# Four modulation jobs of block 2's last layer: from TensorE in block 2 to GpSimd in block 1

## The chip, the core and the metric

The kernel runs on one core of a Trainium2 chip. A core has TensorE (matmuls), VectorE, ScalarE and GpSimd, each with its own in-order queue of instructions, and SyncE, whose queue (SP) issues the DMAs here. The metric is the time of one execution on the device in microseconds; lower is better.

## What is computed

Two blocks of two layers each, on 256 tokens of 1024 features in fp32. Every layer is modulated by a vector `c`: a product of `silu(c)` with a 1024 x 3072 matrix gives shift, scale and gate. Block 1 has one modulation vector, block 2 two (latents and context). Cut to that:

```python
def hybrid_layer(x, c_silu, ...):                       # block 1, 2 layers
    shift, scale, gate = split(c_silu @ w_ada + b_ada, 3)
    u = rms_norm(x, norm_g) * (1 + scale) + shift
    z = u @ w_in                                        # then attentions a, b, c and their merge
    return x + gate * (merged @ w_out)

def mixer_layer(x, cx, c, c_ctx, ...):                  # block 2, 2 layers
    shift, scale, gate = split(silu(c) @ w_ada + b_ada, 3)
    shift_c, scale_c, gate_c = split(silu(c_ctx) @ w_ada + b_ada, 3)
    h = x * (1 + scale) + shift;  hc = cx * (1 + scale_c) + shift_c
    ...                                                 # h @ w_in, four mixers, w_out, layer norm
```

## The kernel before

**Weights.** All projections go through the same path. SP loads half a tile of weights (128 x 1024, 512 KB) into one of three buffers `wr` (`raw`, L222), ScalarE makes its rounded part `wh` (L114) and VectorE the rest `wl` (L115), with four buffers each, and TensorE multiplies three combinations of `wh`, `wl` with the split activations (`mm`, L107).

**Modulation.** The 3072 columns of a layer's modulation are worked out in the background by one of two kinds of jobs (`ada`). A *small job* takes 256 columns (12 to a layer): two loads of 512 KB, eight matmuls `ps<-wsp,cs` or `ps<-wr,cs`, a copy `adas`, two transposes, and two small VectorE instructions into `mod`. A *wide job* takes 512 columns (6 to a layer, so one stands for two small ones) and works on GpSimd: four loads (L324), each of which is multiplied by a column of `cs` (L330, L333) and added up in `acc` (L334); with two modulation vectors that makes 16 multiplications and 14 additions. Its `end` is eight matmuls of `acc` with ones (four with one vector) and one VectorE instruction. The first of the two products of a piece of weights goes into a tile `wc`, the second overwrites the weights. The loads of wide jobs go in turn into the two tiles `t3a` and `t3b` (`N.spare`).

**What sets the order.** The jobs stand in a list `bg`. After each of certain weight tiles (42 in a layer of block 1) `after_tile` adds `N.rate` to `N.due` and, for each whole unit, takes a job from the list, as long as more than `N.hold` are left. `end` of a wide job is put into `later` and run ten `after_tile`s on (six with one vector), or at a `flush`. At the start of layer 1 of block 1 `fill(4, ...)` takes four small jobs at once, whose eight loads go into the tiles `a4`, `a5`, `a6`, `g1`, `g2`, `g3`, `t3a` and `t3b`; they are to lie under the switch of layers. A scheduler then orders the instructions of each engine, so that code order is only a hint; on the chip each engine and SP follow that order strictly.

**The switch between the layers of block 1.** When the last output tile of layer 0 is done, ScalarE squares `xT`, TensorE sums the squares (`th,ones`, then `sel,cs`), VectorE scales the sum (L378), GpSimd takes its power -1/2 (`rc`, L379), VectorE makes a diagonal of it (`dg`, L382), TensorE spreads it (`dg,ones`), and VectorE and ScalarE make the split `u` (L524 to L526), with which the projections of layer 1 begin (`wh,uh`).

**Where the jobs are before.** In layer 0 of block 1: two wide jobs of its own gate and four of layer 1 (one vector each). In layer 1: four wide jobs for layer 0 of block 2. In block 2: the four last small jobs of its layer 0 (two of them at its start), and all twelve of its layer 1, so that 14 go through `wr`. Of the tags: `stg` is the tile in which block 1 stages its `bq` queries (L456); `w2` is used only by layer 1 of block 2.

Of the kernel before, what the change touches and what calls it, by code (L numbers as in the profile page):

```python
# [58 lines left out]
class Net:  # L59
# [185 lines left out]
    def run_later(self, now=False):  # L245

        left = []
        for n, f in self.later:
            if n > 0 and not now:
                left.append((n - 1, f))  # L250
                continue
            with self.tc.issue_after(self.last_mm):
                f()
        self.later = left
# [34 lines left out]
    def ada(self, l, blk):  # L289

        nc = self.nc
        nv = 1 if blk == 1 else 2
        wa = self.I["w_ada" if blk == 1 else "w_ada_2"][l]
        v0 = blk - 1
        mod = self.const.tile([128, 24, nv], F32, name=f"mod{blk}{l}")

        def load(n):
            return [self.raw(wa, k, n * 256, 256, True) for k in (0, 4)]

        def job(n, ws=None):  # L300
            ws = ws or load(n)
            bias = self.colB[:, 48 * (blk - 1) + 24 * l:48 * (blk - 1) + 24 * l + 24]
            p = self.P(self.pj, [128, 512])
            for k in range(8):
                g = 32 * (k % 4)
                self.mm(p[g:g + 32, :256], self.cs[:, k, :], ws[k // 4][:, k % 4, :], start=k < 4, stop=k >= 4)
            sb = self.W("adas", [128, 256], tag="score")
            nc.scalar.activation(sb, p[:, :256], AF.Copy)
            pc = self.P(self.tr, [128, 2, 4, 32])
            for j in range(2):  # L310
                self.T(pc[:, j].rearrange("p g v -> p (g v)"), sb[:, 128 * j:128 * j + 128])
            r = self.W("adar", [128, 2, nv])
            nc.vector.tensor_reduce(r, pc[:, :, :, v0:v0 + nv].rearrange("p j g v -> p j v g"), axis=AX.X, op=OP.add)
            nc.vector.scalar_tensor_tensor(mod[:, 2 * n:2 * n + 2, :], r, 0.5,
                                           bias[:, 2 * n:2 * n + 2][:, :, None].to_broadcast([128, 2, nv]),
                                           op0=OP.mult, op1=OP.add)
        def wide(n, tag):

            P = nc.gpsimd
            acc = self.K("acc", [128, 2, 512], tag=tag)  # L320
            for c in range(4):
                w = self.K("wsp", [128, 2, 512], tag=self.spare[self.nspare % len(self.spare)])
                self.nspare += 1
                nc.sync.dma_start(out=w, in_=wa[256 * c:256 * c + 256, 512 * n:512 * n + 512].rearrange(  # L324
                    "(k p) n -> p k n", p=128))
                for k in range(2):
                    for v in range(nv):
                        m = self.cs[:, 2 * c + k, v0 + v:v0 + v + 1]
                        if c == k == 0:
                            P.tensor_scalar(acc[:, v], w[:, k], m, None, op0=OP.mult)  # L330
                        else:
                            t = self.W("wc", [128, 512], tag="stg") if v + 1 < nv else w[:, k]
                            P.tensor_scalar(t, w[:, k], m, None, op0=OP.mult)  # L333
                            P.tensor_tensor(acc[:, v], acc[:, v], t, op=OP.add)  # L334

            def end():
                p = self.P(self.tr, [128, 4, 32])
                for j in range(4):
                    for v in range(nv):
                        self.mm(p[:, j, v:v + 1], acc[:, v, 128 * j:128 * j + 128], self.ones[:, 0:1])  # L340
                bias = self.colB[:, 48 * (blk - 1) + 24 * l:48 * (blk - 1) + 24 * l + 24]
                nc.vector.scalar_tensor_tensor(mod[:, 4 * n:4 * n + 4, :], p[:, :, :nv], 0.5,
                                               bias[:, 4 * n:4 * n + 4][:, :, None].to_broadcast([128, 4, nv]),
                                               op0=OP.mult, op1=OP.add)
            self.later.append((6 if nv == 1 else 10, end))

        return (mod, [lambda ws=None, n=n: job(n, ws) for n in range(12)], [lambda n=n: wide(n, ("s4", "w1")[n % 2]) for n in range(6)],
                load)

# [991 lines left out]
def build(ctx, tc, I, out):  # L1341
    N = Net(ctx, tc, I)
    nc = N.nc

    def flush(left=0):
        while len(N.bg) > left:
            N.bg.popleft()()
        N.run_later(True)

    N.load_consts()  # L1350
    mod, jobs, wide, load = N.ada(0, 1)
    N.spare = ["t3a", "t3b", "a1", "a2", "a3", "a4", "a5", "a6", "a7", "g1", "g2", "g3", "t1"]
    ws = {0: load(0)}
    N.ident = N.const.tile([128, 128], F32, name="ident")
    nc.sync.dma_start(out=N.ident, in_=I["ident"])
    ws[4] = load(4)
    xT = N.K("xT", [128, 8, 256])
    nc.sync.dma_start(out=xT, in_=I["x"])
    for n in range(4):
        for m in (n, n + 4):  # L1360
            jobs[m](ws.get(m))
    pre = {"idx": [N.raw(N.I["w_in"][0], k, OFF1["idx"], 256) for k in (0, 4)]}
    t = N.K("pre", [128, 8, 256], tag="t2")
    for k in (0, 4):
        nc.sync.dma_start(out=t[:, k:k + 4], in_=N.I["w_in"][0][k * 128:k * 128 + 512, :256].rearrange(
            "(k p) n -> p k n", p=128))
    pre["aq"] = [t[:, 0:4], t[:, 4:8]]
    t = N.K("pre", [128, 8, 68], tag="n2")
    nc.sync.dma_start(out=t, in_=N.I["w_in"][0][:, OFF1["idx"] + 256:OFF1["idx"] + 324].rearrange(
        "(k p) n -> p k n", p=128))  # L1370
    pre["iw"] = [t[:, 0:4], t[:, 4:8]]
    N.load_cs1()
    N.spare = ["t3a", "t3b"]
    N.bg.extend(wide[4:])
    for l in range(2):
        nmod, jobs, wide, _ = N.ada(1, 1) if l == 0 else N.ada(0, 2)
        N.bg.extend(wide[:4] + jobs[8:])
        N.hold = 4
        N.rate = 0.19 if l == 0 else 0.11
        N.due = 1.0  # L1380
        N.block1(l, xT, mod, pre if l == 0 else {})
        flush(4)
        mod = nmod
    X = N.halves("cT", ("t3a", "t3b"))
    for t, ks in X.parts():
        nc.sync.dma_start(out=t, in_=I["ctx_2"][:, ks])
    H, R = {}, {}

    def stream(l, s, x, r, g, b, mod):
        H[s] = N.pair("h" + s, {"x": ("uh", "ul"), "c": ("t1", "t2")}[s])  # L1390
        sc, bi = N.mod_cols(g, b, mod, 0 if s == "x" else 1)
        N.affine_split(H[s][0], H[s][1], x, sc, bi, r)
        if s == "x" or l == 0:
            R[s] = N.residual(x, r, g, b, f"res{s}{l}")

    stream(0, "c", X, None, None, None, mod)
    stream(0, "x", xT, N.rstd_row(xT, EPS), N.colA[:, 0:8], None, mod)
    nmod, jobs, _, _ = N.ada(1, 2)
    N.bg.extend(jobs)
    N.hold = 0  # L1400
    N.rate = 0.8
    ln = lambda l: (N.colA[:, 24 + 8 * l:32 + 8 * l], N.colA[:, 40 + 8 * l:48 + 8 * l])

    def context_done(x, r):
        flush()
        stream(1, "c", x, r, *ln(0), nmod)

    N.spare = None
    N.fill(2, ["a7", "g1", "g2", "g3"])
    x, r = N.block2(0, R, H, mod, context_done)  # L1410
    stream(1, "x", x, r, *ln(0), nmod)
    xT, r = N.block2(1, R, H, nmod, None)
    g, b = ln(1)
    for k in range(8):
        nc.vector.scalar_tensor_tensor(xT[:, k], xT[:, k], g[:, k:k + 1], r, op0=OP.mult, op1=OP.mult)
        nc.scalar.activation(xT[:, k], xT[:, k], AF.Identity, bias=b[:, k:k + 1])
        nc.sync.dma_start(out=out[:, k], in_=xT[:, k])
# [74 lines left out]
```

## Time and profile before

| | |
|---|---|
| median of 3 runs (lowest to highest) | 1353.47 us (1352.70 to 1354.14) |
| the profiled execution, its own time | 1352.58 us |
| its span in the trace | 1350.8 us |
| mean granted clock of TensorE | 0.972 |
| TensorE busy | 1277.5 us (95%) |
| VectorE, ScalarE, GpSimd busy | 908.9, 648.8, 393.9 us |

The span is shorter than the execution's own time, since it begins with the first instruction; differences within the trace are read in the span, and are compared with the times as differences. A busy TensorE says that matmuls were in flight, not that they ran at full speed.

### The profile page before, as it was taken

How to read it: one execution, taken by the hardware profiler on the slowest of the kernel's cores; microseconds unless marked ns; L12 is line 12 of the kernel's file. 1: busy time of each engine (PE TensorE's matmuls, PEld its weight loads, DVE VectorE, ACT ScalarE, POOL GpSimd, SP SyncE). 2: the span in 40 equal slices, each digit the busy share in tenths (PEclk: the TensorE clock that was granted, in tenths of full speed). 3: DMA queues.
4: the chain of work that ended last, by engine and by line, in shares of the span. 5: the costliest groups of instructions: out<-in, count | busy, mean ns of one | idle time of the engine just before them, and what ended most of it. 6: DMA issues, size and time to landing. Idle time of an engine off the chain costs nothing.

```text
span 1350.8 us, 27852 instructions
## 1 busy us (share of the span) xinstructions
PE 1277.5 (95%) x11386; PEld 1163.7 (86%) x11386; DVE 908.9 (67%) x1717; ACT 648.8 (48%) x1160; POOL 393.9 (29%) x233
## 2 busy tenths in 40 slices
PE   6999999999998999999998999999899999999986
PEld 2988988999898898899997988987789789999775
DVE  3897675665679855486675376754748768696873
ACT  3445456644444545764453233334736646434652
POOL 0484984150098921949500010000000000000000
PEclk8899999999989999999998999999899998999997
DMA  9764885476645575446664554326244255654220
GB/s 327 252 203 141 250 244 166 137 243 211 179 143 170 150 209 161 141 155 209 208 208 142 155 157 133 91 94 172 77 142 140 74 161 156 188 159 109 79 79 32
DMA packets 199599, 217.65 MB, mean 161 GB/s; under 512 B 10800, under 2 KB 183472, under 8 KB 198832
## 3 DMA queue, kind: packets, MB, share of 16 engines
q1 hardware_dynamic: 199472, 215.87, 53.2%
q8 instruction: 90, 1.47, 0.5%
q14 instruction: 37, 0.30, 0.1%
HBM read 199.06 MB, written 4.19 MB: 150 GB/s over the span
## 4 chain that ended last, share of the span: by engine, by line
PE 72%; DVE 12%; issue 6%; SPq 4%; DMA 3%; ACT 3%; POOL 0%; POOLq 0%; ACTq 0%; DVEq 0%
PE ps L107 68%; PE ps L111 4%; DVE wl L115 3%; SPq L466 2%; DMA wr<-w_in 2%; SPq L222 1%; DVE pe L703 1%; DVE nm L482 1%; DVE score L589 1%; ACT pe L487 1%; DMA wsp<-w_ada 1%; ACT wh L114 1%; DVE m L588 1%; DVE ro L428 1%; DVE score L584 0%
## 5 line engine op out<-in xcount | busy, mean ns | idle before, releaser
L115 DVE TENSOR_TENSOR wl<-wr,wh 128x1024 fp32r<-128x1024 f32 (+1 forms) x270 | 357.6, 1326 | 226.9 <-ACT wh L114 223.3
L114 ACT ACTIVATE wh<-wr 128x1024 fp32r<-128x1024 f32 (+1 forms) x270 | 284.9, 1056 | 349.3 <-PE ps L107 200.0
L107 PE MATMUL ps<-uh,wh 128*128 128x256 f32 x704 | 201.8, 287 | 3.4 <-ACT thm L659 3.4
L107 PE MATMUL ps<-ul,wh 128*128 128x256 f32 x704 | 201.2, 286 | 0.0
L107 PE MATMUL ps<-uh,wl 128*128 128x256 f32 x704 | 200.7, 285 | 0.0
L333 POOL TENSOR_SCALAR wsp<-wsp,cs 128x512 f32<-128x512 f32 x70 | 137.3, 1967 | 20.9 <-DMA wsp<-w_ada 20.9
L107 PEld LDWEIGHTS ps<-uh,wh 128*128 128x128 f32 x704 | 132.8, 189 | 5.8 <-ACT thm L659 4.4
L107 PEld LDWEIGHTS ps<-ul,wh 128*128 128x128 f32 x704 | 132.7, 188 | 3.1 <-issue 2.9
L107 PEld LDWEIGHTS ps<-uh,wl 128*128 128x128 f32 x704 | 132.8, 189 | 1.5 <-issue 1.1
L107 PE MATMUL ps<-wh,uh 128*128 128x256 f32 (+1 forms) x416 | 121.3, 293 | 1.8 <-ACT uh L525 1.4
L107 PE MATMUL ps<-wl,uh 128*128 128x256 f32 (+1 forms) x416 | 121.0, 292 | 1.5 <-DVE wl L115 1.5
L107 PE MATMUL ps<-wh,ul 128*128 128x256 f32 (+1 forms) x416 | 120.4, 290 | 0.4 <-DVE ul L526 0.4
L334 POOL TENSOR_TENSOR acc<-acc,wsp 128x512 f32<-128x512 f32 x70 | 107.8, 1540 | 2.5
L487 ACT ACTIVATE pe<-ps,nm 128x512 f32<-128x512 f32 (+2 forms) x160 | 85.0, 542 | 42.3 <-DVE nm L482 29.3
L397 POOL TENSOR_TENSOR rec<-rec,mhalf 128x8 f32<-128x8 f32 (+1 forms) x10 | 15.4, 1544 | 293.9 <-DVE rec L396 193.8
L482 DVE TENSOR_REDUCE nm<-ps 128x1 f32<-128x512 f32 (+2 forms) x104 | 70.8, 685 | 26.3 <-PE ps L107 24.7
L107 PEld LDWEIGHTS ps<-wh,uh 128*128 128x128 f32 x416 | 82.1, 198 | 3.7 <-ACT uh L525 1.6
L107 PEld LDWEIGHTS ps<-wl,uh 128*128 128x128 f32 x416 | 82.2, 198 | 2.8 <-DVE wl L115 1.8
L107 PEld LDWEIGHTS ps<-wh,ul 128*128 128x128 f32 x416 | 82.1, 198 | 0.8 <-DVE ul L526 0.7
L379 POOL TENSOR_TENSOR rc<-rc,mhalf 128x2 f32<-128x2 f32 x6 | 5.0, 833 | 255.4 <-DVE rc L378 255.4
L107 PE MATMUL ps<-wl,hxh 128*128 128x256 f32 x256 | 73.2, 286 | 0.5 <-DVE wl L115 0.5
L107 PE MATMUL ps<-wh,hxh 128*128 128x256 f32 x256 | 73.2, 286 | 0.1
(377 smaller groups left out, 3526.3 us busy)
## 6 DMA issues: line engine op xcount, KB each, us to landing
wr<-w_in SPq DMA_DIRECT2D x204, 512.0 KB, 4.1
wsp<-w_ada SPq DMA_DIRECT2D x68, 512.0 KB, 5.0
wr<-w_out SPq DMA_DIRECT2D x40, 512.0 KB, 3.5
wr<-w_ada SPq DMA_DIRECT2D x28, 512.0 KB, 4.5
wr<-w_br_a SPq DMA_DIRECT2D x8, 512.0 KB, 3.6
wr<-w_br_c SPq DMA_DIRECT2D x8, 512.0 KB, 4.0
wr<-w_br_b SPq DMA_DIRECT2D x8, 512.0 KB, 4.3
kC<-stg SPq DMA_DIRECT2D x64, 64.0 KB, 2.1
```

The lines of the kernel that those rows point to most:

```text
L107: self.last_mm = self.nc.tensor.matmul(o, l, r, start=start, stop=stop, skip_group_check=True).ins
L111: self.nc.tensor.transpose(o, i, self.ident[:n, :n])
L114: self.nc.scalar.activation(h, x, AF.Copy)
L115: self.nc.vector.tensor_tensor(l, x, h, op=OP.subtract)
L222: self.nc.sync.dma_start(out=w[:, :, :n], in_=ap[k0 * 128:k0 * 128 + 512, c0:c0 + n].rearrange("(k p) n -> p k n", p=128))
L333: P.tensor_scalar(t, w[:, k], m, None, op0=OP.mult)
L334: P.tensor_tensor(acc[:, v], acc[:, v], t, op=OP.add)
L397: self.nc.gpsimd.tensor_tensor(r, r, self.mhalf[:, :r.shape[1]], op=OP.pow)
L428: V.tensor_tensor(dst, t1, b, op=OP.add)
L466: self.nc.sync.dma_start(out=d[32 * i:32 * i + 32].bitcast(F32), in_=g[32 * j:32 * j + 32, part].bitcast(F32))
L482: nc.vector.tensor_reduce(nmx, p, axis=AX.X, op=OP.max, negate=True)
L487: nc.scalar.activation(e[:, j, :], p[:, j, :], AF.Exp, bias=nm[:, h:h + 1], accum_out=ss[:, h:h + 1])
```

## The change

`ada(1, 2)`, the modulation of the last layer of block 2, is built in front of layer 0 of block 1. Its first two wide jobs follow the four of layer 1 of block 1 on the list of layer 0, and block 2 gets only the small jobs 4 to 11. An entry of `later` now says whether a `flush` may hurry it (`soon`); the `end`s of the two moved jobs may not. `wc` gets a tile of its own, `w2`.

```diff
     def run_later(self, now=False):
 
         left = []
-        for n, f in self.later:
-            if n > 0 and not now:
-                left.append((n - 1, f))
+        for n, f, soon in self.later:
+            if n > 0 and not (now and soon):
+                left.append((n - 1, f, soon))
                 continue
             with self.tc.issue_after(self.last_mm):
                 f()
@@
-                            t = self.W("wc", [128, 512], tag="stg") if v + 1 < nv else w[:, k]
+                            t = self.K("wc", [128, 512], tag="w2") if v + 1 < nv else w[:, k]
@@
-            self.later.append((6 if nv == 1 else 10, end))
+            self.later.append((6 if nv == 1 else 10, end, (l, blk) != (1, 2)))
@@
         nmod, jobs, wide, _ = N.ada(1, 1) if l == 0 else N.ada(0, 2)
-        N.bg.extend(wide[:4] + jobs[8:])
+        if l == 0:
+            last = N.ada(1, 2)
+            wide[4:] = last[2][:2]
+        N.bg.extend(wide[:6 if l == 0 else 4] + jobs[8:])
@@
-    nmod, jobs, _, _ = N.ada(1, 2)
-    N.bg.extend(jobs)
+    nmod, jobs, _, _ = last
+    N.bg.extend(jobs[4:])
```

What this does to the order of the engines is seen at three places around the switch between the layers of block 1. The names carry a number for each use of a tile; what stands in brackets are the queues on which the instruction waits.

GpSimd before, at the end of layer 0: the last wide job of layer 1 (`acc_3128`), then `rc`, then the first wide job for block 2 (`acc_4666`).

```order
L333 TENSOR_SCALAR wsp_3146<-wsp_3146,cs_92 128x512
L334 TENSOR_TENSOR acc_3128<-acc_3128,wsp_3140 128x512 [waits Pool_49]
L334 TENSOR_TENSOR acc_3128<-acc_3128,wsp_3146 128x512 [waits Pool_49] x2
L379 TENSOR_TENSOR rc_4158<-rc_4158,mhalf_91 128x2 [waits DVE_49]
L330 TENSOR_SCALAR acc_4666<-wsp_4667,cs_92 128x512 [waits DMAHW0_49,PE_49]
```

GpSimd now, at the same `rc`: it stands within the second moved job (`acc_3856`), whose third load is `wsp_3878`.

```order
L334 TENSOR_TENSOR acc_3856<-acc_3856,wc_3880 128x512 [waits Pool_49]
L333 TENSOR_SCALAR wsp_3878<-wsp_3878,cs_92 128x512
L379 TENSOR_TENSOR rc_4261<-rc_4261,mhalf_91 128x2 [waits DVE_49]
L333 TENSOR_SCALAR wc_3885<-wsp_3878,cs_92 128x512 [waits Pool_49]
L334 TENSOR_TENSOR acc_3856<-acc_3856,wsp_3878 128x512 [waits Pool_49]
L334 TENSOR_TENSOR acc_3856<-acc_3856,wc_3885 128x512 [waits Pool_49]
L333 TENSOR_SCALAR wsp_3878<-wsp_3878,cs_92 128x512
L333 TENSOR_SCALAR wc_3892<-wsp_3890,cs_92 128x512 [waits DMAHW5_49,Pool_49]
L334 TENSOR_TENSOR acc_3856<-acc_3856,wsp_3878 128x512 [waits Pool_49]
```

Between the last product of `acc_3129` (the former `acc_3128`) and `rc` there are now 47 products, 30 of the first moved job and 17 of the second; six more stand between `rc` and the last reader of `wsp_3878`.

SP now, from the fourth load of the second moved job on; `wsp_4372` and `wsp_4374` are the halves of the last of the four small jobs of `fill`, in the tiles `t3a` (after `wsp_3878`) and `t3b` (after `wsp_3890`). Before, the same two loads (`wsp_4269`, `wsp_4271`) stood some 35 rows earlier, on either side of the last load from `w_br_c`.

```order
L324 DMA wsp_3890<-w_ada_2 128x2x512 [waits Pool_49]
L222 DMA wsp_4372<-w_ada 128x4x256 [waits DMAHW7_49,Pool_49]
L324 DMA wsp_4770<-w_ada_2 128x2x512 [waits DMAHW6_49,PE_49]
L222 DMA wr_4703<-w_in 128x4x256 [waits DMAHW2_49,DVE_49]
L222 DMA wr_4815<-w_in 128x4x256 [waits DMAHW3_49,DVE_49]
L222 DMA wr_4821<-w_in 128x4x256 [waits DMAHW4_49,DVE_49]
L222 DMA wsp_4374<-w_ada 128x4x256 [waits DMAHW5_49,Pool_49]
```

The two loads have moved behind the loads of the moved wide jobs, with a wait for GpSimd.

TensorE before, at the switch: the transposes of two small jobs, the norm's `dg,ones`, one more pair of transposes, and the first matmuls of layer 1.

```order
L111 MATMUL ps_4263<-ident_111,adas_4261 128x128 [waits DVE_49,Activation_49]
L111 MATMUL ps_4263<-ident_111,adas_4261 128x128
L107 MATMUL ps_4155<-dg_4161,ones_90 128x256 [waits DVE_49]
L111 MATMUL ps_4284<-ident_111,adas_4282 128x128 [waits Activation_49]
L111 MATMUL ps_4284<-ident_111,adas_4282 128x128
L107 MATMUL ps_4305<-wh_4294,uh_4172 128x256 [waits Activation_49]
```

TensorE now, at the same place.

```order
L111 MATMUL ps_4366<-ident_111,adas_4364 128x128 [waits DVE_49,Activation_49]
L111 MATMUL ps_4366<-ident_111,adas_4364 128x128
L107 MATMUL ps_4258<-dg_4264,ones_90 128x256 [waits DVE_49]
L107 MATMUL ps_4376<-wsp_4372,cs_92 32x256 [waits DMAHW6_49]
L107 MATMUL ps_4376<-wsp_4372,cs_92 32x256 x3
L107 MATMUL ps_4408<-wh_4397,uh_4275 128x256 [waits Activation_49]
```

The first half of the last small job's matmuls, which were ahead of the norm's `dg,ones`, now stands behind it and ahead of the first matmul of layer 1.

## Rows read from the trace of the kernel before

**Rows 1.** The page: its head and the busy times

```profile
span 1350.8 us, 27852 instructions
PE 1277.5 (95%) x11386; PEld 1163.7 (86%) x11386; DVE 908.9 (67%) x1717; ACT 648.8 (48%) x1160; POOL 393.9 (29%) x233
```

**Rows 2.** Stretches: length, busy us of engines (instructions), granted clock, DMA share, GB/s

```profile
290.00:366.00 76.00, 76.00 (x677) 74.37 (x676) 48.77 (x58) 35.16 (x41) 0.00 (x0) 1.00 0.65 195
...
604.00:660.00 56.00, 56.00 (x480) 55.70 (x480) 36.51 (x34) 22.55 (x26) 54.48 (x28) 1.00 0.63 192
```

**Rows 3.** Timeline of TensorE at the switch: start, us, engine, line, operation

```profile
369.42 0.70 PE L107 MATMUL ps<-dg,ones 128*128 128x256 f32 x2 [0.33 <-DVE dg L382]
...
371.70 0.51 PE L107 MATMUL ps<-wh,uh 128*128 128x256 f32 x2 [1.36 <-ACT uh L525]
```

**Rows 4.** Timeline of GpSimd around the switch; in brackets: idle before, and releaser

```profile
284.76 4.91 POOL L334 TENSOR_TENSOR acc<-acc,wsp 128x512 f32<-128x512 f32 x3
368.12 0.73 POOL L379 TENSOR_TENSOR rc<-rc,mhalf 128x2 f32<-128x2 f32 x1 [78.45 <-DVE rc L378]
370.93 3.41 POOL L330 TENSOR_SCALAR acc<-wsp,cs 128x512 f32<-128x512 f32 x2 [2.08 <-DMA wsp<-w_ada]
...
414.71 4.24 POOL L330 TENSOR_SCALAR acc<-wsp,cs 128x512 f32<-128x512 f32 x2 [0.34 <-DMA wsp<-w_ada]
```

**Rows 5.** Timeline of SP, the DMA queue, at four places

```profile
286.08 0.37 SPq L222 DMA_DIRECT2D wsp<-w_ada  x1
...
314.14 8.21 SPq L222 DMA_DIRECT2D wr<-w_br_b  x4
...
381.05 1.82 SPq L222 DMA_DIRECT2D wr<-w_in  x2
...
996.89 7.06 SPq L222 DMA_DIRECT2D wr<-w_ada  x2
```

**Rows 6.** DMA issues, 280 to 380 us: count, KB each, median us to landing

```profile
wsp<-w_ada SPq DMA_DIRECT2D x6, 512.0 KB, 4.6
```

**Rows 7.** Timeline of GpSimd: first and last product of two wide jobs

```profile
535.72 1.57 POOL L333 TENSOR_SCALAR wc<-wsp,cs 128x512 f32<-128x512 f32 x1 [47.63 <-DMA bq<-stg]
...
582.85 2.59 POOL L333 TENSOR_SCALAR wsp<-wsp,cs 128x512 f32<-128x512 f32 x1
604.25 3.11 POOL L330 TENSOR_SCALAR acc<-wsp,cs 128x512 f32<-128x512 f32 x2 [18.81 <-PE ps L107]
...
657.60 1.30 POOL L334 TENSOR_TENSOR acc<-acc,wsp 128x512 f32<-128x512 f32 x1
```

**Rows 8.** Stretches, TensorE on `wr` alone: one small job's matmuls

```profile
860.00:900.00 40.00, 1.07 (x16) 0.96 0.45 127
```

**Rows 9.** Stretches, TensorE alone, behind the switch: length, busy (matmuls), clock

```profile
371.69:380.03 8.34, 7.89 (x51) 0.80 0.00 0
```

**Rows 10.** The tile `wsp`: its loads from issue to landing

```profile
DMA to landing us min/median/max: 3.6/5.0/11.5
```

**Rows 11.** Groups of instructions, TensorE: busy us and mean ns of the `end` matmuls

```profile
L107 PE MATMUL ps<-ones,acc 128*128 128x1 f32 x112 | 13.3, 244 | 0.0
```

**Rows 12.** Timeline of TensorE in block 2: the transposes of a small job

```profile
728.48 0.38 PE L111 MATMUL ps<-ident,adas 128*128 128x128 f32 x2
```

**Rows 13.** Stretches, TensorE alone, where the last four small jobs lie

```profile
873.00:1012.00 139.00, 127.66 (x1045) 0.95 0.41 118
```

**Rows 14.** Waits of TensorE, 885 to 1068 us: total, times, longest

```profile
PE ps L107 <- ACT wh L114: 0.7, 1, 0.7
...
PE ps L111 <- DVE adar L313: 0.9, 1, 0.9
```

**Rows 15.** Groups of VectorE, splits of weights: 290 to 366, then 604 to 660

```profile
L115 DVE TENSOR_TENSOR wl<-wr,wh 128x1024 fp32r<-128x1024 f32 x27 | 33.9, 1257 | 19.9 <-ACT wh L114 19.7
...
L115 DVE TENSOR_TENSOR wl<-wr,wh 128x1024 fp32r<-128x1024 f32 x17 | 26.8, 1585 | 16.4 <-ACT wh L114 16.4
```

**Rows 16.** The chain of waits in block 2: start, us, what

```profile
1004.04 4.58 DMA wr<-w_out
```

## The prediction, written before the run

> **What bounds the kernel now.** I read the page first: in a span of 1350.8 us TensorE is busy for 95% [rows 1], so an edit is worth what TensorE gains or loses by it. Then I read the two stretches that the change touches, by engine. In the last 76 us of layer 0 of block 1 TensorE is busy in all 76.00 us while GpSimd does nothing, and in the same stage of layer 1 it is busy in 56.00 of 56 us while GpSimd works through 54.48 [rows 2]. Products on GpSimd can therefore run under that stage. What does not run under anything is the switch between the two layers: TensorE does its last matmul of the norm at 369.42 us and starts the first projection of layer 1 at 371.70 [rows 3]. Ahead of that stands one GpSimd instruction, `rc` (L379), which runs at 368.12, as soon as VectorE has made its input; GpSimd had been idle since 289.67 us (284.76 + 4.91) and starts its next products at 370.93 [rows 4]. In the change GpSimd is not idle there.
>
> **The change, part by part.** The sum is made against the profiled execution (1352.58 us); the median of the runs is 0.9 us above it.
>
> *The wide jobs at the layer switch.* The two wide jobs are taken up at the 32nd and the 37th of the 42 weight tiles of layer 0 at which the list is looked at, with four loads and 30 products each. By the order of GpSimd, 47 of these 60 products stand ahead of `rc`, and six more between `rc` and the last reader of `wsp_3878`. The load of `wsp_4372`, one of the two halves of the weights of a small job of block 1, goes into the tile that `wsp_3878` leaves, and on TensorE the four matmuls that read it stand directly ahead of the first matmul of layer 1. So the first projection waits for 47 products, `rc`, six products, a load and four matmuls, in this sequence.
>
> When does it begin? The first load of the moved jobs stands where `wsp_4269`, in the same tile, was loaded before: at 286.08 us [rows 5]. Such loads land after a median of 4.6 us in this stretch [rows 6], so GpSimd starts at 290.7. The tiles come free in time for the later loads, so GpSimd then runs on. What does a product cost? Its spans overlap, so I take start to start: 30 products with 29 steps between 604.25 and 657.60 give 1.84 us, between 535.72 and 582.85 1.63 [rows 7]; at the start of layer 1, 26 steps from 370.93 to 414.71 give 1.68 [rows 4]. The first of these is the same stage (merging and its splits), one layer later, so 1.84 it is: 47 x 1.84 = 86.5, so `rc` starts at 377.2 instead of 368.12 and ends, 0.73 later [rows 4], at 377.9. Six products at the 1.68 of the switch: 388.0. The load: 392.6. A small job has 16 matmul records in 1.07 us at full clock [rows 8]; half of them at the half clock, to which TensorE falls when it has idled (the mean granted clock of the 8.34 us after the switch is 0.80 [rows 9]), is 1.1: 393.7. Against 371.70 that is **+22.0 us**.
>
> Something comes back: the affine steps of `u`, between which the first 51 matmuls now trickle in 8.34 us [rows 9], are all done by then. At the pace of the full stage, 76.00 us for 677 matmuls [rows 2], 51 take 5.7; of the difference of 2.6 I take half, since the clock has to rise again: **-1.3** (bounds 0 and -2.6).
>
> Bounds of the stall: at 1.63 us a product GpSimd is through at 367.3 and `rc` runs at 368.12 as before, but six products (9.8), a load at its fastest of 3.6 [rows 10] and 0.5 of matmuls still follow: 382.8, or +11.1. At the highest mean that a stage shows, 54.48 us busy for 28 products, 1.95 [rows 2], and a load of 5.0 [rows 10], it is 400.9, or +29.2. No bound is zero: the order alone puts six products and a load between `rc` and the projection.
>
> *The two `end`s of the wide jobs.* Each has 8 matmuls, and such matmuls cost 13.3 us for 112 records, 0.12 each [rows 11]. 16 records are 1.9 us. The first `end` lies in the wait of the switch and costs nothing; without that cover it would be 1.9. The second lies in the projections: **+1.9** (0 to 3.8 for both).
>
> *The four small jobs gone from block 2.* A job's 1.07 us of matmuls [rows 8] and its two transposes of 0.38 together [rows 12] make 1.45; four make **-5.8**. In the place of the last four, 873 to 1012 us, TensorE is busy in 127.66 of 139 us [rows 13], so most of it is seen. Lower bound: nothing, if the jobs only filled its gaps. Upper bound: in that stretch TensorE waits 0.7 us for a split of weights and 0.9 for a job's reduction [rows 14], 1.6 that may go with the jobs: -7.4.
>
> *The product tile `w2`.* `wc` no longer shares `stg` with the staging of `bq`, so the 47.63 us that GpSimd waits ahead of 535.72 [rows 7] go. TensorE did not wait for that job, so it is worth nothing; the third wide job of layer 1 only starts earlier.
>
> The sum: 22.0 - 1.3 + 1.9 - 5.8 = +16.8, 1369.4 us for a profiled execution, **1370 us** for the median.
>
> **The rivals.**
>
> *VectorE becomes the bound (slower still).* Every split on VectorE reads two tensors from SBUF, and its mean rises from 1257 ns without GpSimd to 1585 with it [rows 15]. By these rows the 27 splits of the stage cost 27 x 0.33 = 8.9 us more, on an engine with 48.77 us of work in 76 [rows 2]: hidden. If each of them instead waited out a whole GpSimd product of 1.84 us, VectorE would need 48.77 + 27 x 1.84 = 98.5 us in 76, and TensorE would be late by some 22 us; about half of that would hide in the wait for GpSimd that follows: 1381. Against it: in the same stage of layer 1 TensorE loses nothing. The Trainium skill (SBUF — State Buffer, section "Who interferes with whom") states that such an instruction and a GpSimd one exclude each other for the whole instruction, whichever starts first; by that rule the worst case is the 1381 above, and the trace agrees with the direction, not with the size (0.33 us a split). 0.04.
>
> *The weights come late (slower still).* SP issues in order, and a load of a moved job that waits for GpSimd holds back what is behind it. The fourth load of the first job waits for 15 products, to 318.3, in the midst of the `w_br_b` loads that begin at 314.14 [rows 5]: some 2 us. `wsp_4372` holds SP to 388; but before, too, SP issues the next weights only at 381.05 [rows 5], 9.4 us after TensorE has started, since the buffers are full. If a hold did get through it would add some 5 us: 1375. 0.04.
>
> *The low end of everything (about the same).* A stall of 11.1 - 2.6, no cost of the ends and 7.4 gained: +1.1, 1354.6. It needs GpSimd at 1.63 us a product under the splits of the merge. With its neighbours within 2.7 us: 0.06.
>
> *Block 2 gains more than its matmuls (faster).* The last small job's two loads take buffers of the weight ring at 996.89 [rows 5], ahead of `w_out`, for which the chain waits 4.58 us at 1004.04 [rows 16]. If that wait goes with the jobs, block 2 gains 7.4 + 4.6 = 12.0, which decides once the stall is below that: with 8.5 it comes to -3.5, 1350. Against it: over the whole of 885 to 1068 us TensorE itself idles only 0.7 us for a split [rows 14], so the chain's wait is mostly under other matmuls. 0.06. That the jobs do not leave block 2 at all is excluded by its order, in which ten pairs of `w_ada` loads into `wr` stand where there were fourteen.
>
> **How the numbers follow.** The forecast, a stall at the switch that outweighs block 2, has the remaining 0.80, and 1370. A measurement of this kernel can tell 0.2% (2.7 us) from no change. Slower 0.80 + 0.04 + 0.04 = 0.88, same 0.06, faster 0.06. The range for 8 in 10 leaves out the faster case, most of the same and the upper ends: 1357 to 1382. Below, that is a stall of 11.1 with the upper bound of the gain in block 2 (1370 - 10.9 - 1.6); above, a stall of 29.2 (1377) with some of the lower bound of that gain.
>
> **What would show it.** In the profile after: GpSimd busy without a gap from about 291 us; `rc` at about 377, released by GpSimd's own queue rather than by VectorE; TensorE idle for about 13 us between the `dg` matmul and the `wsp,cs` matmuls, with the load of `wsp` from `w_ada` named as the releaser, and the first `wh,uh` of layer 1 at about 394; TensorE as full as before up to 366; from 700 on everything later by the stall and the gap to before closing by some 6 us between 870 and 1012. The prediction is wrong if GpSimd's products run at 1.5 us or less, if TensorE does not stand behind that load, or if block 2 gains 12 us or more.

## The result, and the profile after

The changed kernel takes **1373.7 us** (median of three runs, 1368.05 to 1375.48) against 1353.47 before: a ratio of 1.0134, 95% interval 1.0112 to 1.0156, which of 1353 us is +18.1 (15.2 to 21.1); the two medians by themselves lie 20.2 us apart. The forecast was 1370 and slower. The profiled execution is the one of 1375.48 us, the slowest of the three. Its page, head and busy times:

```profile
span 1373.4 us, 27836 instructions
PE 1283.2 (93%) x11346; PEld 1170.1 (85%) x11346; DVE 919.9 (67%) x1711; ACT 646.7 (47%) x1156; POOL 506.9 (37%) x293
```

TensorE is busy 5.7 us longer than in [rows 1] although it has fewer instructions, and GpSimd 113 us longer. The place to look first is the switch. GpSimd there (timeline, as in [rows 4]):

```profile
289.84 3.69 POOL L330 TENSOR_SCALAR acc<-wsp,cs 128x512 f32<-128x512 f32 x2 [0.75 <-PE ps L107]
...
358.45 1.57 POOL L333 TENSOR_SCALAR wc<-wsp,cs 128x512 f32<-128x512 f32 x1 [1.20 <-DMA wsp<-w_ada]
...
379.14 0.73 POOL L379 TENSOR_TENSOR rc<-rc,mhalf 128x2 f32<-128x2 f32 x1
...
387.38 1.26 POOL L334 TENSOR_TENSOR acc<-acc,wsp 128x512 f32<-128x512 f32 x1
```

It works from 289.84 on with one gap of 1.20 us, and `rc` has no idle time ahead of it: it stands in GpSimd's queue. The chain of waits from there (start, us, what):

```profile
379.18 0.71 POOL rc L379
...
388.67 3.56 DMA wsp<-w_ada
392.23 0.04 issue
392.27 23.03 PE ps L107 x167
```

and TensorE's timeline, which answers to [rows 3]:

```profile
380.88 1.22 PE L107 MATMUL ps<-dg,ones 128*128 128x256 f32 x2 [5.53 <-DVE dg L382]
392.27 1.08 PE L107 MATMUL ps<-wsp,cs 128*32 128x256 f32 x8 [10.17 <-DMA wsp<-w_ada]
393.28 0.58 PE L107 MATMUL ps<-wh,uh 128*128 128x256 f32 x1
```

The last reader of the tile ends at 388.64, the load is issued at 388.67, the four matmuls (eight records) start at 392.27, and the first projection starts at 393.28 instead of 371.70: 21.6 us late. TensorE waits 5.53 us for `dg` and 10.17 for the load, 15.7 together. The other 5.9 were lost earlier. The step of VectorE that makes `rc`'s input (L378) starts at 373.79 us; before, it started at 367.88:

```profile
373.79 0.16 DVE L378 TENSOR_SCALAR rc<-ps 128x2 f32<-128x2 f32 x1
```

So the last stage of layer 0 had lost time too. The stretches (columns as in [rows 2], whose first one answers to the first):

```profile
290.00:366.00 76.00, 73.81 (x597) 73.29 (x597) 55.38 (x54) 31.42 (x36) 74.72 (x39) 0.96 0.70 217
...
334.00:350.00 16.00, 13.81 (x90) 13.29 (x89) 15.26 (x14) 6.45 (x9) 16.00 (x9) 0.79 0.64 200
```

and the same 16 us in the kernel before:

```profile
334.00:350.00 16.00, 16.00 (x138) 16.00 (x137) 11.79 (x15) 6.80 (x8) 0.00 (x0) 1.00 0.56 169
```

Busy time alone shows a loss of 2.19 us there. The number of matmuls shows more: 90 instead of 138, and at 16.00/138 = 0.116 us each the 48 missing are 5.6 us. The rest of the loss is in the clock column, 0.79: behind a short wait TensorE runs at the lower of its two levels for a while. Count matmuls, not busy time, where that column is under 1.

How late the stage is, is better read from a mark in the same execution. The `end` of the last wide job for layer 1 (eight records of `ones,acc`, within layer 0) serves as one; before, then after, with the first moved `end` (16 records) as the third line:

```profile
310.15 0.95 PE L107 MATMUL ps<-ones,acc 128*128 128x1 f32 x8
```

```profile
309.57 0.95 PE L107 MATMUL ps<-ones,acc 128*128 128x1 f32 x8
...
367.19 1.84 PE L107 MATMUL ps<-ones,acc 128*128 128x1 f32 x16
```

From the mark to L378 the kernel before takes 57.73 us (310.15 to 367.88), and so do, to 0.01, the profiles of runs 3, 4, 6, 11 and 12 below, which move no job into layer 0. The mark itself lies anywhere from 310.09 to 314.33 in them, so plain starts in two profiles compare to some 4 us only. The change takes 64.22: its stage loses 6.5 us. The 5.6 of missing matmuls and 1.8 for the first moved `end`, which stands ahead of the norm's sums, less 1.1 for the last small job's matmuls, which stood ahead of L378 before and no longer do, make 6.3 of it.

After the switch the delay stays what it is: +23.4 us at `rc` of block 2 (734.36 instead of 710.93), +22.6 at the end of the span. From end to end block 2 gave back nothing that can be seen.

### The profile page after: what moved, and what is told of

It reads as the page before. It is cut to its first block, busy times and chain, and to the rows that moved or that the text cites. A ratio compares the mean times of both kernels' runs of the same rounds, so it can differ in the third digit from the quotient of the medians.

```text
span 1373.4 us, 27836 instructions
## 1 busy us (share of the span) xinstructions
PE 1283.2 (93%) x11346; PEld 1170.1 (85%) x11346; DVE 919.9 (67%) x1711; ACT 646.7 (47%) x1156; POOL 506.9 (37%) x293
## 4 chain that ended last, share of the span: by engine, by line
PE 66%; DVE 9%; POOL 8%; DMA 6%; issue 5%; ACT 3%; SPq 2%; POOLq 0%; ACTq 0%; DVEq 0%
PE ps L107 63%; DMA wr<-w_in 4%; PE ps L111 4%; POOL acc L334 3%; POOL wsp L333 2%; DMA wsp<-w_ada 2%; DVE wl L115 2%; POOL wc L333 2%; DVE nm L482 1%; SPq L222 1%; ACT wh L114 1%; SPq L466 1%; DVE pe L703 1%; ACT pe L487 1%; POOL acc L330 1%
## 5 line engine op out<-in xcount | busy, mean ns | idle before, releaser
L115 DVE TENSOR_TENSOR wl<-wr,wh 128x1024 fp32r<-128x1024 f32 (+1 forms) x270 | 363.7, 1348 | 237.3 <-ACT wh L114 228.4
L333 POOL TENSOR_SCALAR wsp<-wsp,cs 128x512 f32<-128x512 f32 x84 | 175.0, 2089 | 18.0 <-DMA wsp<-w_ada 18.0
L334 POOL TENSOR_TENSOR acc<-acc,wsp 128x512 f32<-128x512 f32 x84 | 128.2, 1526 | 2.5
L333 POOL TENSOR_SCALAR wc<-wsp,cs 128x512 f32<-128x512 f32 x42 | 79.7, 1897 | 18.8 <-DMA wsp<-w_ada 18.8
L330 POOL TENSOR_SCALAR acc<-wsp,cs 128x512 f32<-128x512 f32 x18 | 32.0, 1785 | 140.7 <-PE ps L107 111.1
L397 POOL TENSOR_TENSOR ssq<-ssq,mhalf 128x8 f32<-128x8 f32 x3 | 4.9, 1649 | 204.3 <-DVE ssq L396 143.4
```

Of the source, the lines that this page charges most:

```text
L115: self.nc.vector.tensor_tensor(l, x, h, op=OP.subtract)
L397: self.nc.gpsimd.tensor_tensor(r, r, self.mhalf[:, :r.shape[1]], op=OP.pow)
```

## The experiments

The differences of the first four are against 23 executions of the kernel before (median 1351.3), of the next four against 10 (1352.7; an eleventh, of 6039 us, is left out), of the last four against 12 (1353.5). Microseconds behind a ratio are of 1353.

**1. The last small job's loads in tiles that don't wait for GpSimd.**

```diff
-            self.fill(4, ["a4", "a5", "a6", "g1", "g2", "g3", "t3a", "t3b"])
+            self.fill(4, ["a4", "a5", "a6", "g1", "g2", "g3", "a1", "a2"])
```

> The change, with the two loads of block 1's last small job in tiles that do not wait for GpSimd; the rest as in the change. If the wait at the layer switch is a chain of 47 GpSimd products, `rc`, six products, a load and four matmuls, the second half of that chain goes: the first projection follows `rc` (about 379 us) by the affine steps alone, so it starts 11 to 13 us earlier than in the change, and the kernel takes about 1362 us (1359 to 1365), still some 9 us over before. If the time was lost to contention of GpSimd with VectorE's splits, or to weights that SP holds back, nothing of it goes: 1372 to 1375.

Measured: 1369.3 us, ratio 1.0141 (1.0116 to 1.0167), +19 us: no gain. The theory's number fails. Its trace shows that the wait for the load is gone, and what stands in its place (VectorE, then TensorE):

```profile
384.65 2.50 DVE L382 TENSOR_SCALAR dg<-ident,rc 128x128 f32<-128x128 f32 x2 [2.93 <-POOL rc L379]
```

```profile
387.20 1.22 PE L107 MATMUL ps<-dg,ones 128*128 128x256 f32 x2 [6.83 <-DVE dg L382]
390.15 0.79 PE L107 MATMUL ps<-wh,uh 128*128 128x256 f32 x2 [1.73 <-ACT uh L525]
```

GpSimd's order has 48 products ahead of `rc` here, one more, and `rc` comes at 383.88. Then the two instructions of `dg` take 2.50 us beside GpSimd's products, where they took 0.48 before and 0.92 in the change. The first projection comes 3.1 us earlier than in the change instead of 11 to 13 (6.1 if both are counted from the mark, which lies at 312.50 here). L378 comes at 378.19, which from the mark is 1.5 later than in the change. Two waits that follow each other do not add: with one gone, the steps that had been hidden under it were late themselves.

**2. The moved jobs taken up earlier.**

```diff
-        N.rate = 0.19 if l == 0 else 0.11
+        N.rate = 0.25 if l == 0 else 0.11
```

> The change, with the wide jobs of layer 0 of block 1 taken up at a rate of 0.25 a tile instead of 0.19, so that GpSimd has all 60 added products behind it before `rc` of layer 1. Just as much GpSimd work runs beside TensorE's stages. If the loss is the queue of products in front of `rc`, all of the stall goes and what is left is the `end`s' 1.9 us and what block 2 gives back: 1347 to 1356. If GpSimd's work beside VectorE, its loads or the missing jobs in block 2 cost the time, the kernel stays at 1368 to 1375.

Measured: 1368.1 us, 1.0115 (1.0087 to 1.0142). The queue ahead of `rc` is gone and the time is not. GpSimd at the switch (timeline):

```profile
385.81 0.73 POOL L379 TENSOR_TENSOR rc<-rc,mhalf 128x2 f32<-128x2 f32 x1 [10.51 <-DVE rc L378]
```

GpSimd had been idle 10.51 us, and `rc` waits for VectorE as it did before, but 17.7 us later. So all the loss is now ahead of `rc`, in TensorE's last stage of layer 0. Its timeline, and a stretch around the line (the kernel before has 138 matmuls there):

```profile
321.87 3.14 PE L107 MATMUL ps<-ones,acc 128*128 128x1 f32 x14 [3.29 <-POOL acc L334]
```

```profile
318.00:334.00 16.00, 12.71 (x75) 12.62 (x75) 3.48 (x4) 3.28 (x4) 13.39 (x9) 0.68 0.53 165
```

The `end` of a wide job waits 3.29 us for its products, and the 63 matmuls that are missing there are 7.3 us.

**3. The product tile alone.**

```diff
-                            t = self.W("wc", [128, 512], tag="stg") if v + 1 < nv else w[:, k]
+                            t = self.K("wc", [128, 512], tag="w2") if v + 1 < nv else w[:, k]
```

> The kernel before, with GpSimd's second product in the tile w2 and nothing else. By the prediction it is worth nothing (1353.5, within 2.7): the 47 us that GpSimd waits ahead of 535.72 us go, but TensorE does not wait for that job. The rival: a third wide job that starts earlier in layer 1 runs beside more splits or holds `rc` of block 2, and the time moves by 3 us or more.

Measured: 1352.4 us, 1.0004 (0.9989 to 1.0019): nothing, as forecast. The stretch in which the job now runs (GpSimd is the fifth engine; it was busy 12.70 us there before):

```profile
470.00:520.00 50.00, 50.00 (x417) 48.35 (x418) 28.88 (x25) 25.01 (x31) 47.69 (x27) 1.00 0.71 214
```

GpSimd's wait went and TensorE, full in those 50 us, is not touched.

**4. Four small jobs of block 2 left out.**

```diff
-    N.bg.extend(jobs)
+    nc.vector.memset(nmod[:, 0:8], 0.0)
+    N.bg.extend(jobs[4:])
```

> The kernel before, with the first four small jobs of block 2's last layer left out and done nowhere (the modulation's first 8 columns are zero there), to measure what their leaving gives in block 2 without any GpSimd work. The prediction's term: 5.8 us (0 to 7.4), so about 1347.7. The rival that the trace of the change suggests: TensorE's time in block 2's first layer is set by something else than its number of matmuls, and no more than 1.5 us is gained (1352 or more). A gain of 10 or more would be the load on the chain that goes with the jobs.

Measured: 1350.6 us, 0.9997 (0.9981 to 1.0014): 0.4 us gained, with bounds of -1.9 and 2.6. The 5.8 of the prediction lies outside. One profiled execution could not have told this: TensorE's order up to block 2 is that of before in this kernel, and yet its `rc` of block 2 lies 5.3 us later than that of the profile before (716.2 and 710.93); from there to the end it takes 5.7 less. The tile-alone run, with the full list of jobs, takes 3.7 less over the same part.

**5. One wide job moved instead of two.**

```diff
-            wide[4:] = last[2][:2]
-        N.bg.extend(wide[:6 if l == 0 else 4] + jobs[8:])
+            wide[4:] = last[2][:1]
+        N.bg.extend(wide[:5 if l == 0 else 4] + jobs[8:])
...
-    N.bg.extend(jobs[4:])
+    N.bg.extend(jobs[2:])
```

> The change with one wide job moved instead of two, so 33 added products and not 47 to 60 ahead of `rc`, and two small jobs fewer in block 2 instead of four. GpSimd has nothing to do from 289.7 to 368.1 us before, 78 us; 33 products at 1.84 us are 61. If the loss comes from GpSimd having more than it has room for ahead of the layer switch, nothing of it is left and the time is that of before, 1349 to 1354. If every product costs TensorE something (contention, held weights), half of the loss stays: about 1362.

Measured: 1367.1 us, 1.0101 (1.0075 to 1.0127), +13.6 us. Half the work costs three quarters of the loss; that GpSimd merely has too much to do is refuted. The trace shows two things, on ScalarE and on GpSimd:

```profile
345.44 1.06 ACT L114 ACTIVATE wh<-wr 128x1024 fp32r<-128x1024 f32 x1 [7.68 <-DMA wr<-w_out]
```

```profile
381.54 3.10 POOL L330 TENSOR_SCALAR acc<-wsp,cs 128x512 f32<-128x512 f32 x2 [28.55 <-DMA wsp<-w_ada]
384.61 1.57 POOL L333 TENSOR_SCALAR wc<-wsp,cs 128x512 f32<-128x512 f32 x1
386.14 0.74 POOL L379 TENSOR_TENSOR rc<-rc,mhalf 128x2 f32<-128x2 f32 x1
```

A split waits 7.68 us for `w_out`, and L378 comes at 379.02, 11.1 us late. And GpSimd is idle for 28.55 us and still holds `rc` back: the first three products of layer 1's next wide job now stand ahead of it in the order, and their load is late. Free time on an engine does not help an instruction that stands behind another one's wait. From the mark (312.69) to L378 the stage loses 8.6 us of the 11.1.

**6. All twelve small jobs left out, and 12. eight of them.**

```diff
-    N.bg.extend(jobs)
+    nc.vector.memset(nmod, 0.0)
```

```diff
-    N.bg.extend(jobs)
+    nc.vector.memset(nmod[:, 0:16], 0.0)
+    N.bg.extend(jobs[8:])
```

> The kernel before with all 12 small jobs of block 2's last layer left out and done nowhere (its modulation is zero there): the price of a small job in block 2 with three times the lever of leaving out four. The prediction's price of 1.45 us each: 17.4 us, so about 1335. If the jobs only fill time in which TensorE waits anyway, as leaving out four suggests (0.8 +- 2.3 us): no more than 5 us, 1347 or more.

> The kernel before with the first eight small jobs of block 2's last layer left out and done nowhere (16 of its modulation's 24 columns are zero): between four (0.4 us gained, -1.9 to 2.6) and twelve (15.8, 11.8 to 19.8). If the jobs have one price, the twelve give 1.3 us each and eight give 10.5: 1342. If the last places in the list are free and the first ones not, eight give 3 to 7: 1346 to 1350.

Measured: twelve out, 1336.1 us, 0.9883 (0.9853 to 0.9913), 15.8 us gained; eight out, 1341.0 us, 0.9908 (0.9886 to 0.9930), 12.5 gained (9.5 to 15.4). At the prediction's 1.45 us a job these would be 17.4 and 11.6, and both intervals hold that. So the price of a job is right and the gain is not in proportion: 0.4, 12.5 and 15.8 us for four, eight and twelve. The theory that the last places in the list are free, which gave eight jobs 3 to 7 us, falls. Why the first four bring nothing stays open.

**7. `rc` off GpSimd's queue.**

```diff
-        self.nc.gpsimd.tensor_tensor(c, c, self.mhalf[:, :2], op=OP.pow)
+        V.tensor_scalar(c, c, 0.0, 0.5, op0=OP.mult, op1=OP.add)
...
-            self.fill(4, ["a4", "a5", "a6", "g1", "g2", "g3", "t3a", "t3b"])
+            self.fill(4, ["a4", "a5", "a6", "g1", "g2", "g3", "a1", "a2"])
```

> The change with `rc` on VectorE and without its power (so the scale of the norm is a constant there, which changes values and no shape), and with the last small job's loads in tiles that do not wait for GpSimd: TensorE has no wait for GpSimd's queue left at the layer switch, and all 60 products run as in the change. If that queue is the main part of the loss, `dg` follows VectorE's step at about 374 us, the first projection at about 378 instead of 394, and the kernel takes 1356 to 1360: what stays is the 5.9 us by which the last stage of layer 0 ends late in the change. If GpSimd beside VectorE sets the pace of the affine steps too: 1364 or more.

`V` is VectorE; the power is left out here. Measured: 1362.6 us, 1.0073 (1.0044 to 1.0101), +9.9. The wait for the queue was worth some 8 of the change's 18 us (18.1 less 9.9, each known to 3 or 4, so the 8 to some 5). The time lies between the two expectations, and the trace says why: VectorE's step ahead of the switch, and TensorE's first projection.

```profile
378.71 0.16 DVE L378 TENSOR_SCALAR rc<-ps 128x2 f32<-128x2 f32 x1 [1.18 <-PE ps L107]
```

```profile
384.43 0.79 PE L107 MATMUL ps<-wh,uh 128*128 128x256 f32 x2 [1.36 <-ACT uh L525]
```

L378 starts 10.8 us late here and not 5.9, but 3.2 of it lie ahead of the mark (313.33): the stage loses 7.7 us, where it lost 6.5 in the change. Counted from the mark the first projection is 9.6 us late. The kernel is 9.9 us slower by the ratio; the profiled execution, the fastest of the six (1358.88 us), is 6.2 over the median of before.

**8. The four small jobs kept in block 2 as well.**

```diff
-    N.bg.extend(jobs[4:])
+    N.bg.extend(jobs)
```

> The change with the four small jobs done in block 2 as well (their results are written twice, the same): the change's cost without its gain. By the prediction's term the gain is 5.8 us, so this takes about 1379 if the change takes 1373 and 1375 if it takes 1369. If the jobs cost block 2 nothing: as the change, within 2 us.

Measured: 1368.0 us, 1.0120 (1.0091 to 1.0150). With four jobs more it is not slower than the change; that they brought the change 5.8 us is not borne out here either.

**9. The moved jobs' loads on GpSimd's own queue.** To the kernel of 7:

```diff
-                nc.sync.dma_start(out=w, in_=wa[256 * c:256 * c + 256, 512 * n:512 * n + 512].rearrange(
+                (P if (l, blk) == (1, 2) else nc.sync).dma_start(out=w, in_=wa[256 * c:256 * c + 256, 512 * n:512 * n + 512].rearrange(
```

> The run with `rc` off GpSimd (1362.6 us, ratio 1.0073), and in it the eight loads of the two moved wide jobs issued from GpSimd's own queue, so that SP no longer stands behind a tile that GpSimd holds. If the 9 us that are left there are weights of `w_br_b` and `w_out` that come late because of SP, and the lowered clock after the wait for them, they go: 1352 to 1356. If they are contention of products with VectorE, or the second `end`, they stay: 1360 or more.

Measured: 1359.2 us, 1.0044 (1.0020 to 1.0068), +6.0; the runs lie between 1353.3 and 1365.6, and the profile is that of the slowest. In it SP issues the first `w_out` at 328.88 and all eight without a `wsp` load between them, so nothing of GpSimd holds SP; what that brought over run 7, 3.9 us, is not certain, since the two intervals overlap. The stage still ends late: L378 at 377.54, 7.8 us more than before from the mark (312.01). Its waits of TensorE from 325 to 366 us, the groups of VectorE's splits from 325 to 368, and a stretch:

```profile
PE ps L107 <- DVE wl L115: 2.6, 1, 2.6
```

```profile
L115 DVE TENSOR_TENSOR wl<-wr,wh 128x1024 fp32r<-128x1024 f32 x13 | 24.2, 1873 | 3.2 <-ACT wh L114 3.1
L115 DVE TENSOR_TENSOR mgl<-mga,mgh 128x512 fp32r<-128x512 f32 x4 | 4.1, 1054 | 0.0
...
340.00:350.00 10.00, 7.04 (x42) 6.66 (x41) 9.97 (x9) 2.33 (x4) 9.96 (x7) 0.74 0.40 119
```

VectorE (third) is busy in 9.97 of 10 us and TensorE waits for a split. From 340 to 360 us there are 122 matmuls instead of 174, 6.0 us at 0.116 each; the other 1.8 of the 7.8 are the first moved `end`, which stands ahead of the norm's sums here too (at 370.14). The same two groups in the kernel before, and in the change:

```profile
L115 DVE TENSOR_TENSOR wl<-wr,wh 128x1024 fp32r<-128x1024 f32 x14 | 17.0, 1224 | 7.8 <-ACT wh L114 7.5
L115 DVE TENSOR_TENSOR mgl<-mga,mgh 128x512 fp32r<-128x512 f32 x4 | 2.7, 685 | 0.0
```

```profile
L115 DVE TENSOR_TENSOR wl<-wr,wh 128x1024 fp32r<-128x1024 f32 x14 | 22.0, 1581 | 10.3 <-ACT wh L114 10.1
L115 DVE TENSOR_TENSOR mgl<-mga,mgh 128x512 fp32r<-128x512 f32 x4 | 4.2, 1057 | 0.0
```

**10. Earlier, on GpSimd's queue, with later `end`s.** To the kernel of 2, the loads as in 9, and `end` after 16 tiles:

```diff
-            self.later.append((6 if nv == 1 else 10, end, (l, blk) != (1, 2)))
+            self.later.append((6 if nv == 1 else 16 if l else 10, end, (l, blk) != (1, 2)))
```

> The earlier wide jobs of the second experiment (1368.1 us, ratio 1.0115), with their loads on GpSimd's own queue and their `end`s 16 tiles after the job instead of 10. There TensorE lost 17.7 us before `rc`, by its trace in a wait for the products at an `end` and in late weights, each followed by a stretch at the lower clock. If these two are all, it comes to the time of before, 1349 to 1355, with the right result. If GpSimd beside VectorE costs by itself, or the loads from GpSimd are slow, 1360 or more.

Measured: 1363.7 us, 1.0080 (1.0064 to 1.0096), +10.8. No wait for an `end` is left, SP issues the eight `w_out` loads in one piece from 329.35 on, some 5 us are gained on run 2, and the dip of run 9 is there (besides it, TensorE waits 2.11 us at 381.58 for a small job's load, ahead of `dg,ones`):

```profile
340.00:350.00 10.00, 7.19 (x43) 6.41 (x43) 9.97 (x10) 2.75 (x4) 10.00 (x6) 0.78 0.50 157
```

**11. The wide jobs in block 2 instead.** The kernel before, product tile and loads as above, and

```diff
-    N.bg.extend(jobs)
+    N.bg.extend(jobs[:2] + jobs[4:6] + jobs[8:])
...
     N.fill(2, ["a7", "g1", "g2", "g3"])
+    N.spare = ["t3a", "t3b"]
+    wide[1]("s4", 5)
+    wide[3]("w1", 8)
+    N.spare = None
```

(the second argument is the number of tiles until `end`; these two stand for the small jobs 2, 3, 6 and 7, not for the change's first four).

> The kernel before, with the two wide jobs done by GpSimd in block 2's first layer, where it is idle (11 us busy of 320), in place of the same four small jobs; loads on GpSimd's queue, products' tile w2. If four small jobs fewer are worth something when no switch stands behind the products: 1346 to 1350. If the last four places are worth nothing, as leaving them out said, and the small steps of norms on GpSimd (`rec`) now stand behind products: 1353 to 1362.

Measured: 1381.5 us, 1.0215 (1.0190 to 1.0239), +29: slower than any other, where GpSimd had been idle. TensorE's waits from 700 to 900 us:

```profile
PE ps L107 <- DVE QTc L918: 7.9, 3, 2.9
PE ps L107 <- ACT hxh L525: 5.1, 2, 2.9
PE ps L107 <- DVE dg L382: 3.5, 1, 3.5
PE ps L111 <- DVE ro L426: 3.0, 1, 3.0
```

They name short steps of VectorE, or steps fed by it; before, the waits in that window are 10.7 us in all. `rc` alone stands behind products for 3.5 us (714.43 for 710.93). No version that does all the work was found faster than before.

## Why the prediction was right, and where it was not

**The stall at the switch: the right steps, with a price that was right by luck.** Start of GpSimd 290.7 forecast, 289.84 measured; 47 products by 377.2, measured 379.14, so 1.90 us each from the first one and not 1.84; the last reader through at 388.0, measured 388.64; the load in at 392.6, measured 392.2; the first projection at 393.7, measured 393.28. The term was +22.0 and is +21.6. But the 1.84 is a miscount: between 604.25 and 657.60 us lie 28 products, as [rows 2] says (x28), and not 30, since two products of that job ran ahead of the first row [rows 7], the one at 582.85 among them. With 27 steps a product costs 1.98, and the same sum gives +28.4. And the errors that are left cancel: `rc` came 1.9 late, but the six products took 8.8 us instead of 10.1 and the load 3.56 instead of 4.6. The matmuls behind it come faster than in [rows 9], as forecast (TensorE alone, columns as there):

```profile
393.27:400.70 7.43, 7.43 (x56) 0.80 0.36 99
```

51 of these 56 take 6.8 us instead of 8.34, 1.5 less where 1.3 was taken. That the queue costs time is shown by run 7, at some 8 of the 18 us; without it the stage in front, late as well, sets the rest. Run 1 shows that the first half of the chain is enough for the loss.

**"The weights come late": it happened, and did not count.** The prediction gave it 0.04, put the fourth load's wait at 318.3 and said that a hold which got through would add some 5 us. SP's timeline in the change, which answers to the `w_br_b` row of [rows 5]:

```profile
315.17 0.37 SPq L222 DMA_DIRECT2D wr<-w_br_b  x1
320.50 0.37 SPq L324 DMA_DIRECT2D wsp<-w_ada  x1
320.95 2.24 SPq L222 DMA_DIRECT2D wr<-w_br_b  x3
...
329.40 1.51 SPq L222 DMA_DIRECT2D wr<-w_out  x2
334.79 0.37 SPq L324 DMA_DIRECT2D wsp<-w_ada  x1
335.25 15.72 SPq L222 DMA_DIRECT2D wr<-w_out  x6
```

The load waits until 320.50, `w_out` starts at 329.40 (324.83 before) and its third tile at 335.25, and TensorE then waits for ScalarE's `wh` (waits of TensorE, 290 to 368 us; before has none there):

```profile
PE ps L107 <- ACT wh L114: 1.9, 1, 1.9
```

With the clock behind it that is most of the 6.5 us that the stage loses. In the sum it is nothing, since GpSimd's queue ends later still. It is part of why runs 1 and 5 gained so little, and run 7 not more: take the longer of two chains away and the shorter one shows.

**"VectorE becomes the bound": the argument against it failed.** The prediction said that in the same stage of layer 1 TensorE loses nothing beside GpSimd [rows 2]. The stretch was the wrong one. In layer 1 GpSimd's last product starts at 657.60 [rows 7], and the merge's splits, which layer 0 has from 333.58 on, come later (VectorE, kernel before):

```profile
674.79 0.68 DVE L115 TENSOR_TENSOR mgl<-mga,mgh 128x512 fp32r<-128x512 f32 x1
```

So no row of before shows the merge beside GpSimd. Runs 9 and 10 do, without a wait for the queue, for SP's hold or for an `end`: splits of 1873 ns instead of 1224 in run 9, 0.65 us more each where 0.33 was taken, a full VectorE, and a dip that costs 6.0 us of matmuls in the profile, the slowest of its runs. Run 9's time is 6.0 us (2.7 to 9.2) over before, which has to hold the moved `end`s too; that VectorE is the cause of the dip is argued from its rows, not isolated. The Trainium skill (SBUF — State Buffer, section "Who interferes with whom") states that a VectorE instruction with two inputs in SBUF contends with a GpSimd one that reads SBUF, and that ScalarE waits for neither. The trace agrees: the mean of the splits on VectorE over the whole kernel goes from 1326 to 1348 ns and ScalarE's stays (groups, after; before it has 1056):

```profile
L115 DVE TENSOR_TENSOR wl<-wr,wh 128x1024 fp32r<-128x1024 f32 (+1 forms) x270 | 363.7, 1348 | 237.3 <-ACT wh L114 228.4
L114 ACT ACTIVATE wh<-wr 128x1024 fp32r<-128x1024 f32 (+1 forms) x270 | 284.8, 1055 | 381.4 <-PE ps L107 211.9
```

**The four small jobs: the term that was mis-sized.** -5.8 was forecast with a lower bound of nothing "if the jobs only filled its gaps"; measured alone it is -0.4 (-2.6 to +1.9), the lower bound. The price of a job holds for eight and for twelve. The profiles hint at where it goes: the change's delay (starts of VectorE's L396 against before) grows from 23.5 us at 794.53 to 27.8 at 901.53 and falls to 24.5 at 1051.59. Between the last two marks, where the jobs lay, it falls by 3.3, in run 4 by 4.1, in run 3, with all jobs, by 0.2, in run 8, with all jobs, by 2.0. So part of the gain is seen in its place and is lost elsewhere in block 2; these are single profiles, and the cause stays open.

**What would show it**, of the prediction's list: GpSimd's run without a gap (but for 1.20 us), `rc` released by its own queue, TensorE's wait with the load named (15.7 us in two waits, some 13 forecast) and the place of the first projection came; TensorE full up to 366 did not come, and the gap closed by some 3 us instead of 6 and had opened by 4 just before. The first is the two rivals above, the late weights and VectorE; the second is the term of the small jobs.

**The two `end`s**, +1.9, are too small to be seen in the time beside an uncertainty of 3 us. The trace shows that the first does not lie in the wait of the switch, as the prediction had it, but ahead of the norm (367.19, 1.84 us); it costs nothing in the change, where GpSimd's queue ends later, and in run 9, without that queue, it is 1.8 of the 7.8 us that the stage loses. **The product tile** was worth nothing, as said (run 3).

Put together, 21.6 - 1.5 and nothing from block 2 is 20.1, and 18.1 (15.2 to 21.1) was measured. The forecast of 16.8 lies within that, in part by luck. With run 4's 0.4 in place of the 5.8 its sum is 22.2; with the products counted right as well, 28.6.

## What to carry to other kernels

An instruction of an engine that stands on the path must be counted with the whole queue ahead of it, its waits included: a short `rc` behind 47 products, or behind three whose load is late, costs as much as they do. Before a queue is shortened, ask which chain ends next; here three of them (GpSimd's queue, SP behind GpSimd's tile, VectorE beside GpSimd) ended within some 15 us of each other, and each repair showed the next. And compare like with like: to say that an engine's work is free under a stage, the row has to show that work under the same instructions.

## What the runs showed that was not expected

A wait of TensorE cost more than twice its length in a full stage: 2.19 us of idle time in the 16 us at 334 became 5.6 us of matmuls at a granted clock of 0.79, and in run 2 3.29 us became 7.3 at 0.68. Beside GpSimd short VectorE instructions can lengthen more than the splits, and unevenly: the two of `dg` took 0.48 us without it and 0.60, 0.92, 1.94 and 2.50 us with it (in run 9, in the change, in runs 5 and 11, and in run 1). And executions of one program differ by more than one reads from a profile: 23 of the kernel before lie between 1346.7 and 1355.5 us, and parts with the same order of instructions up to 5 us apart.
